# A two-layer attention trunk on one core: a shorter weight scale, a joint maximum over three window groups, and group 2 in pairs of tiles z and z+4

## The chip, the cores and the metric

The kernel runs on one core of one Trainium2 chip. The core has five engines, each with its own queue that is worked off in order: TensorE (PE, matrix products into PSUM), VectorE (DVE), ScalarE (ACT), GpSimd (POOL) and SyncE (SP), which issues nearly all DMAs. An instruction waits at the head of its queue until the semaphores it needs are there, and everything behind it waits too. The metric is device time in microseconds (us) of one execution, lower is better.

## What is computed

A trunk of two layers over 1024 positions of width 1024, with 16 heads of 64. Each layer normalises x, projects it to q, k, v and a gate, attends, multiplies by silu(gate), projects back and adds x. Layer 1 is "forgetting attention" (fox); layer 2 attends in dilated windows, three groups with dilations 1, 4 and 16, and weighs the groups by a softmax over their log-sum-exps.

```python
def reference(x, positions, norm_g, ...):
    cos, sin = rotary_tables(positions)
    for i in range(DEPTH):                       # DEPTH = 2
        h = rms_norm(x, norm_g[i])
        if i % 2 == 0: o, gate = fox_mixer(h, ...)
        else:          o, gate = dsw_mixer(h, cos, sin, ...)
        x = x + (o * silu(gate)) @ w_out

def dsw_mixer(...):      # per group g: q, k = rotary(rms_norm(q)), rotary(rms_norm(k))
    o_g, lse_g = dilated_window_attention(q_g, k_g, v_g, window, dilation)
    wts = softmax(stack(lses), axis=0)
    o = einsum('gbsh,gbshd->bshd', wts, stack(outs))
```

Products are made in float16 with a hi and a lo part of each factor: `xh*wh + xh*wl + xl*wh`, three matmuls for each slice of 128 along the contracted width.

## The kernel before

**Blocks and tiles.** The weights of a projection come in blocks of 384 columns (two heads' q, k and v) by 1024 rows. A block meets the eight tiles of 128 rows of x in `project`, 24 matmuls a tile, into one of three PSUM banks named `pj`. Two tiles make a pair. Layer 1 has three gate blocks, eight of q, k, v and three of the output; layer 2 three gate blocks, then 24 of q, k, v (eight of group 0, then for each of eight head pairs one of group 2 and one of group 1) and three of the output.

**Weights.** A block's weights arrive as four float32 tiles `raw` (L270). `bound` (L272 and on) makes a bound on each: the maximum on DVE for even tiles (L281), the sum of squares on ACT for odd ones (L279, into the scrap tile `jk`); ACT brings both to one tile `vm2` (L284, L285). `scale` (L287 to L304) sums the bounds over the partitions by a matmul (L252, L254), clips (L255), takes the root of a power of two by three integer operations (`root_floor`, L241 to L243), then limits the scale from both sides and tracks the smallest one in `low` (L293 to L300). `split` makes the float16 parts: hi on ACT (L310), lo on DVE (L311); the fourth tile is scaled on POOL (L313), cast on ACT (L314) and its lo part made on POOL (L315).

**The chain of a pair.** After `project` fills a bank, DVE copies q and k to `u` (L433), ACT squares them (L438), ACT and DVE take v to hi and lo (L443, L444); L444 is the last reader and sets the bank free. Then, for the pair: DVE sums the squares (L451) and adds the epsilon (L453, `rs_v`); ACT takes logarithm, exponential and square (L471 to L473), DVE refines the root (L474, L475) and multiplies `u*y` (L477); POOL turns the rotary part (L465 to L468). ACT casts the hi part of the float16 tile `hl` (L479), POOL makes the lo part (L480), DVE copies (L481), and SP sends the whole through a transposing DMA into `qk_t` (L485). There is one `hl`, so the cast also waits for the transposing DMA of the pair before. PE makes the scores of the pair from `qk_t` (L505) 16 slots (two pairs of tiles) after its projection, and its values another 16 slots later (fewer at the end).

**Scores to output in layer 2.** `dsw_pair` masks a score and takes its row maximum in one DVE pass (L970), ACT takes the exponential with that maximum (L971) and casts it (L975), POOL makes the lo part (L976), SP transposes it (L977, `ptt`). Groups 0 and 2 write their unnormalised outputs with the maxima to DRAM (`og_d`, L1083). Group 1 loads them back (`load_cmb`, L1037, L1041), weighs them by their maxima (`weigh`: `mm` on DVE L998, then L1000 to L1004 on POOL and ACT) and combines (`combine`, L1011 to L1019).

**What sets the order.** PE's order is written out by hand: `Flow` holds a queue of slots (four a tile) at which scores, values, loads, bounds, scales and splits come due. The other engines' orders are laid out by the framework's scheduler, which places each instruction where it expects it to be ready; a pair's chain has a raised priority. So a change to what is ready when can change the order of other instructions on the same engine.

## Time and profile before

| | us |
|---|---|
| median of 3 runs (1823.03 to 1827.61) | 1825.76 |
| the profiled execution | 1813.33 |
| its span | 1811.5 |
| PE busy | 1659.2 (92%) |
| DVE busy | 1259.9 (70%) |
| ACT busy | 1068.3 (59%) |
| POOL busy | 872.5 (48%) |

The span runs from the first to the last instruction that the profile holds. The stages of the span are: start and fox gates to 200 us, fox blocks to 570, output of layer 1 and gates of layer 2 to 830, group 0 to 1130, groups 2 and 1 to 1720, output to the end. In the last but one stage a group 2 and a group 1 block together take about 76.6 us. Times of single instructions below are counted from the start of the span. A row of a timeline gives start, length, engine, source line, operation, tiles and shape, and in brackets how long the engine idled before it and what ended that.

### The profile page before, as it was taken

The numbers are of one execution on the slowest core, as the hardware profiler recorded it, in microseconds if no ns is written. First come the engines' busy times: TensorE is split into PE (matmuls) and PEld (weight loads), VectorE is DVE, ScalarE is ACT, GpSimd is POOL, SyncE is SP. The second block draws the span as 40 slices with busy tenths as digits, with TensorE's granted clock in tenths as the row PEclk, the third lists the DMA queues.
The fourth block names the chain that finished last, engine by engine and source line by source line (L and its number), as shares of the span: only waits on it lengthen the run. The fifth ranks groups of instructions, "written<-read, shape, count | busy, mean of one in ns | idle before, by whom it ended". The sixth has DMA issues, their size and how long they took to land.

```text
span 1811.5 us, 38107 instructions
## 1 busy us (share of the span) xinstructions
PE 1659.2 (92%) x13342; PEld 1060.2 (59%) x13342; DVE 1259.9 (70%) x3906; ACT 1068.3 (59%) x2790; POOL 872.5 (48%) x1019
## 2 busy tenths in 40 slices
PE   5899898898888997999999989999899998999999
PEld 3566566566665433756666656656556565565654
DVE  8866677766776557766677786677776777767752
ACT  6555666666666546555666666556555565655630
POOL 4203555555554323125565545556475665646520
PEclk8999999999999998999999999999999999999999
DMA  7334998988889777336777787678676777767742
GB/s 260 122 138 103 191 192 174 168 171 195 191 174 209 205 218 225 109 108 139 141 151 168 149 185 152 138 150 164 153 154 141 157 154 158 161 140 153 190 125 91
DMA packets 658769, 292.88 MB, mean 162 GB/s; under 512 B 510208, under 2 KB 622848, under 8 KB 658576
## 3 DMA queue, kind: packets, MB, share of 16 engines
q1 hardware_dynamic: 658576, 290.44, 69.8%
q8 instruction: 104, 1.70, 0.4%
q14 instruction: 89, 0.73, 0.1%
HBM read 124.35 MB, written 41.22 MB: 91 GB/s over the span
## 4 chain that ended last, share of the span: by engine, by line
PE 36%; DVE 12%; DMA 11%; POOL 5%; issue 5%; ACT 3%; SPq 0%; DVEq 0%; POOLq 0%; ACTq 0%
PE pj L345 24%; PE pj L369 8%; DMA qk_t<-hl 6%; PE s L505 2%; DMA raw<-in_w_dsw 2%; DVE p L970 2%; DVE w L311 2%; DVE hl L481 1%; POOL hl L480 1%; POOL ph L976 1%; DVE pj L451 1%; POOL cmb L1003 1%; DMA ptt<-ph 1%; DVE vm L281 1%; POOL raw L313 1%
## 5 line engine op out<-in xcount | busy, mean ns | idle before, releaser
L345 PE MATMUL pj<-w,xh 128*128 128x384 f16 (+2 forms) x4864 | 1191.2, 329 | 32.7 <-DVE vt L444 18.3
L345 PE MATMUL pj<-w,xl 128*128 128x384 f16 (+2 forms) x2432 | 799.1, 329 | 4.8 <-DVE xl L898 2.6
L345 PEld LDWEIGHTS <-xh 128*128 128x128 f16 x4864 | 473.8, 99 | 322.5 <-issue 48.1
L345 PEld LDWEIGHTS <-xl 128*128 128x128 f16 x2432 | 241.4, 99 | 166.7 <-issue 10.6
L552 POOL TENSOR_TENSOR ph<-p,ph 128x512 f16<-128x512 f32 (+3 forms) x176 | 179.1, 1036 | 190.8 <-ACT ph L549 181.3
L480 POOL TENSOR_TENSOR hl<-u,hl 128x512 f16<-128x512 f32 x128 | 153.9, 1203 | 131.5 <-ACT hl L479 131.3
L976 POOL TENSOR_TENSOR ph<-p,ph 128x768 f16<-128x768 f32 (+2 forms) x96 | 154.0, 1604 | 119.4 <-ACT ph L975 116.1
L505 PE MATMUL s<-qk_t 128*128 128x128 f16 (+1 forms) x1504 | 162.9, 249 | 51.2 <-DMA qk_t<-hl 40.1
L311 DVE SCALAR_TENSOR_TENSOR w<-raw,ws_f,w 128x768 f16<-128x768 f32 (+2 forms) x133 | 181.5, 1379 | 9.6 <-ACT w L310 9.5
L369 PE MATMUL pj<-xh,w 128*128 128x512 f16 x512 | 162.0, 386 | 0.0
L505 PEld LDWEIGHTS <-qk_t 128*128 128x128 f16 x1504 | 113.6, 99 | 70.8 <-DMA qk_t<-hl 44.4
L479 ACT CAST hl<-u 128x512 f16<-128x512 f32 x128 | 78.8, 616 | 120.0 <-DMA qk_t<-hl 90.0
L444 DVE SCALAR_TENSOR_TENSOR vt<-pj,vt 128x128 f16<-128x128 f32 x256 | 73.3, 289 | 109.1 <-ACT vt L443 107.1
L438 ACT ACTIVATE sq<-pj 128x256 f32<-128x256 f32 x256 | 96.2, 376 | 76.7 <-DVE u L433 68.0
L546 ACT ACTIVATE p<-p,acc 128x512 f32<-128x512 f32 (+2 forms) x192 | 108.1, 608 | 36.0 <-DVE acc L745 33.2
L560 PEld LDWEIGHTS <-ptt 128*128 128x128 f16 x1136 | 106.9, 99 | 38.1 <-DMA ptt<-ph 26.0
L369 PEld LDWEIGHTS <-w 128*128 128x128 f16 x768 | 75.2, 100 | 86.2 <-issue 7.0
L549 ACT CAST ph<-p 128x512 f16<-128x512 f32 (+3 forms) x176 | 87.7, 537 | 64.2 <-DMA ptt<-ph 63.8
L310 ACT ACTIVATE w<-raw,ws_f 128x768 f16<-128x768 f32 (+2 forms) x133 | 116.9, 911 | 13.7 <-DVE ws_f L293 13.7
L279 ACT ACTIVATE jk<-raw 128x768 f16<-128x768 f32 (+2 forms) x88 | 72.3, 821 | 85.5 <-DMA raw<-in_w_dsw 43.6
L465 POOL TENSOR_TENSOR ra<-u,cs 128x128 f32<-128x128 f32 x96 | 50.3, 524 | 148.7 <-DVE u L433 69.8
L433 DVE TENSOR_TENSOR u<-pj,gr 128x256 f32<-128x256 f32 x256 | 106.2, 415 | 17.2 <-PE pj L345 16.9
(212 smaller groups left out, 2916.5 us busy)
## 6 DMA issues: line engine op xcount, KB each, us to landing
raw<-in_w_dsw SPq DMA_DIRECT2D x96, 384.0 KB, 3.9
raw<-in_w_fox SPq DMA_DIRECT2D x32, 384.0 KB, 4.2
og_d<-og SPq DMA_DIRECT2D x64, 132.0 KB, 2.8
cmb<-og_d SPq DMA_DIRECT2D x64, 132.0 KB, 2.8
bc<-c_d SPq DMA_DIRECT2D x32, 256.0 KB, 4.6
gs_d<-ge SPq DMA_DIRECT2D x32, 192.0 KB, 2.1
xt<-in_xt SPq DMA_DIRECT2D x16, 256.0 KB, 3.8
gsf<-gs_d SPq DMA_DIRECT2D x64, 64.0 KB, 2.5
```

Of the source, the lines that this page charges most:

```text
L310: nc.scalar.activation(w[:, 0, :, :n], raw, AF.Copy, scale=self.sw)
L311: nc.vector.scalar_tensor_tensor(w[:, 1, :, :n], raw, self.sw, w[:, 0, :, :n], ALU.mult, ALU.subtract)
L345: nc.tensor.matmul(ps[:, :n], a[:, k, cols], w.slab(k, j), start=(k == 0 and i == 0), stop=(k == KT - 1 and i == 2))
L369: nc.tensor.matmul(ps[m], w.slab(k, j)[:, m * P : (m + 1) * P], a[:, k, 512 * b : 512 * (b + 1)], start=(k == 0 and x == 0), stop=(k == KT ...
L433: nc.vector.tensor_mul(u[:, t % 2].rearrange("p (a b) d -> p a b d", a=2), ps[:, : 4 * HD].rearrange("p (a b d) -> p a b d", a=2, b=2), gr ...
L438: nc.scalar.activation(sq[:, t % 2], ps[:, : 4 * HD], AF.Square)
L480: nc.gpsimd.tensor_sub(hl[:, :, :4, 1], u, hl[:, :, :4, 0])
L505: nc.tensor.matmul(s[:, c0 : c0 + cnt * P].rearrange("p (c s) -> p c s", c=cnt), qk[:, i, blk], kk[:, j : j + cnt, e], start=(h == 0), sto ...
L546: nc.scalar.activation(p, p, AF.Exp, bias=acc, scale=-1.0)
L552: (nc.gpsimd if pool_l else nc.vector).tensor_sub(ph[:, e, 1, cols], p, ph[:, e, 0, cols])
L560: nc.tensor.matmul(o[:, e, :], hi, vt[:, j, e, HD:], start=(b == 0), stop=False, skip_group_check=True)
L976: nc.gpsimd.tensor_sub(ph[:, 1], st["p"], ph[:, 0])
```

## The change

- **Scale.** Five small DVE operations a block in place of eight or nine: sum, three integer operations, and one that limits the scale between two numbers that are made once a layer (`lim`). The smallest scale is now taken at the end over all of them (`sws`) and not as a running minimum. ACT writes its bounds straight to `vm2`, and the cast L285 goes.
- **Root.** ACT's logarithm reads the sums of squares in PSUM with scale and bias, not DVE's `rs_v` (which is still made).
- **Gates.** One DVE operation makes the gate's product and its maximum; before there were two.
- **Layer 2.** Group 1's exponentials take the joint maximum of the three groups (`joint_most`), so group 1's output needs no weight of its own and `wt` has two groups. In `combine` the gate is multiplied by the reciprocal of the denominator on POOL (on DVE for the last pair of heads), and two DVE products go. The loads of the other groups' outputs stand nine slots earlier, from two slots after the scores to seven before; `cmb` has four buffers and `gsd` four of its own.
- **Group 2's tiles** are worked in the order 0, 4, 1, 5, 2, 6, 3, 7, so that a write to `og_d` has 256 rows of 132 numbers in place of 128 of 264.

```diff
+def nth_tile(g, t):
+    return t // 2 + 4 * (t % 2) if g == 2 else t
...
-    def root_floor(q):
+    def root_scale(dst, q, k):
         e = q.bitcast(I32)
         nc.vector.tensor_scalar(e, e, 1, 0x7FC00000, ALU.logical_shift_right, ALU.bitwise_and)
-        nc.vector.tensor_scalar(e, e, float(127 << 22), None, ALU.add)
-        nc.vector.tensor_single_scalar(e, e, 0x7F800000, ALU.bitwise_and)
-        return e
+        nc.vector.tensor_scalar(e, e, -1.0, float((k << 23) - (127 << 22)), ALU.mult, ALU.add)
+        nc.vector.tensor_single_scalar(dst.bitcast(I32), e, 0x7F800000, ALU.bitwise_and)
...
-            e = root_floor(spread_sums(self.vm2, KT // 2, 2.0 ** -40, 2.0 ** 60))
...
+            root_scale(f[:, 0:1], spread_sums(self.vm2, KT // 2), 268)
             if self.kind == "qkv":
-                nc.vector.tensor_scalar(t2, self.sw, by[:, ly], 2.0, ALU.mult, ALU.max)
-                nc.vector.tensor_scalar(self.sw, t2, 2.0 ** 30, isx[:, ly], ALU.min, ALU.mult)
-                nc.vector.tensor_scalar(t2, t2, 2.0 ** 30, None, ALU.min)
...
-                nc.vector.tensor_tensor(low[:, ly], low[:, ly], self.sw, ALU.min)
...
+                nc.vector.tensor_scalar(self.sw, f[:, 0:1], m[:, 0:1], m[:, 1:2], ALU.max, ALU.min)
+                nc.scalar.activation(self.eps, self.sw, AF.Square, scale=m[:, 2:3])
...
-        nc.scalar.activation(r, v, AF.Ln)
+        nc.scalar.activation(r, w["ss"], AF.Ln, scale=1.0 / HD, bias=w["eps"])
...
-                nc.vector.scalar_tensor_tensor(e, e, w.inv, ps, ALU.mult, ALU.mult)
-                nc.vector.tensor_reduce(peak[:, layer, h * NT + t : h * NT + t + 1], e, AX.X, ALU.max, apply_absolute_value=True)
+                nc.vector.tensor_tensor_reduce(e, e, ps, w.inv, 0.5, ALU.mult, ALU.max, peak[:, layer, h * NT + t : h * NT + t + 1])
...
-                    nc.scalar.activation(p[:, e], p[:, e], AF.Exp, bias=acc[:, e : e + 1], scale=-1.0)
+                    if joint is None:
+                        nc.scalar.activation(p[:, e], p[:, e], AF.Exp, bias=acc[:, e : e + 1], scale=-1.0)
+            if joint is not None:
+                mm = joint().rearrange("p (i e) -> p i e", e=2)
+                for i in range(2):
+                    p = st["p"][:, at[i] : at[i + 1]].rearrange("p (e k) -> p e k", e=2)
+                    for e in range(2):
+                        nc.scalar.activation(p[:, e], p[:, e], AF.Exp, bias=mm[:, i, e : e + 1], scale=-1.0)
...
+    def joint_most(cmb):
+        nm = cmb[0].rearrange("p g t e d -> p g (t e) d")[:, :, :, 65]
+        mm = cmb[3] = sm.tile([P, N2], F32, name="mm", tag="mm")
+        nc.vector.tensor_reduce(mm, nm.rearrange("p g n -> p n g"), AX.X, ALU.min)
+        return mm
...
-        nc.vector.tensor_mul(o, o, cmb[2][:, 0].unsqueeze(2).broadcast_to([P, N2, HD + 1]))
         nc.vector.tensor_add(o, o, cmb[0][:, 1, :, :, : HD + 1].rearrange("p t e d -> p (t e) d"))
         den = sm.tile([P, N2], F32, name="den", tag="den")
         nc.vector.reciprocal(den, o[:, :, HD])
-        y = o[:, :, :HD]
-        nc.vector.tensor_mul(y, y, den.unsqueeze(2).broadcast_to([P, N2, HD]))
+        (nc.vector if hp == NHP - 1 else nc.gpsimd).tensor_mul(gv, gv, den.unsqueeze(2).broadcast_to([P, N2, HD]))
...
-        nc.vector.tensor_mul(y2, y, gv)
+        nc.vector.tensor_mul(y2, o[:, :, :HD], gv)
...
-                dsw_pair(g, t0, qks, vt, done, get, LSD, LPD)
-                flow.at(flow.now + LSD + 2, lambda hp=hp, t0=t0, cmb=cmb: load_cmb(hp, t0, cmb))
+                flow.at(flow.now + LSD - cfg["lcm"], lambda hp=hp, t0=t0, cmb=cmb: load_cmb(hp, t0, cmb))
+                dsw_pair(g, t0, qks, vt, done, get, LSD, LPD, lambda cmb=cmb: joint_most(cmb))
```

The new code also shifts instructions in the queues. First ACT in a group 1 block of layer 2. The block after it has its weights split here: `w<-raw` are the hi parts, `vt<-ws_f` (after: `vt<-sws`) writes a constant column once a block, `hl<-u` is the cast of a pair's q and k. Before:

```order
L443 ACTIVATE vt<-pj 128x2x64
L310 ACTIVATE w<-raw,ws_f 128x768
L299 ACTIVATE ws_f<-ws_f 128x1
L517 ACTIVATE vt<-ws_f 128x16
L479 CAST hl<-u 128x2x4x64
L314 CAST w<-raw 128x768
L310 ACTIVATE w<-raw,ws_f 128x768 x2
```

After, from the last two hi parts to the cast of the same pair (`rs_y<-rs_y` and `pj<-rs_y` are its exponential and square, `jk` the square passes over the weights loaded next, `p<-p,mm` the next pair's exponentials):

```order
L311 ACTIVATE w<-raw,sws 128x768 x2
L480 ACTIVATE rs_y<-rs_y 128x8
L481 ACTIVATE pj<-rs_y 128x8
L445 ACTIVATE sq<-pj 128x256
L283 ACTIVATE jk,vm_18692<-raw 128x768 x2
L288 ACTIVATE vm_18692<-vm 128x2
L985 ACTIVATE p<-p,mm 128x128 x2
L985 ACTIVATE p<-p,mm 128x256 x2
L450 ACTIVATE vt<-pj 128x2x64
L1019 ACTIVATE wt<-wt 128x8
L487 CAST hl<-u 128x2x4x64
```

The cast moved from right behind the first hi part to behind all hi parts, both square passes and the next pair's exponentials.

DVE at the same place. Before, from the running minimum of the scale (`low`) through the pair's `u*y` (L477) to the first two lo parts of the weights (L311):

```order
L300 TENSOR_TENSOR low<-low,ws_f 128x1
L475 SCALAR_TENSOR_TENSOR pj<-pj,rs_y 128x8
L477 TENSOR_TENSOR u<-u,pj 128x512
L444 SCALAR_TENSOR_TENSOR vt<-pj,vt 128x2x64
L311 SCALAR_TENSOR_TENSOR w<-raw,ws_f,w 128x768
L433 TENSOR_TENSOR u<-pj,gr 128x256
L1011 TENSOR_TENSOR ob<-ob,wt 128x260
L311 SCALAR_TENSOR_TENSOR w<-raw,ws_f,w 128x768
```

After, the rows that end with the same pair's `u*y` (L485); its three lo parts of the weights (L312) and the first two score passes stand ahead of them:

```order
L977 ISA p,cmb<-s_17794,band 128x256
L977 ISA cmb 128x1
L977 ISA p,cmb<-s_17794,band 128x256
L977 ISA cmb 128x1
L1031 RECIPROCAL den<-ob 128x4
L458 TENSOR_REDUCE pj<-sq 128x8
L483 SCALAR_TENSOR_TENSOR pj<-pj,rs_y 128x8
L285 TENSOR_REDUCE vm<-raw 128x1
L1011 TENSOR_REDUCE mm<-cmb 128x4
L461 TENSOR_SCALAR rs_v<-pj,ws_f 128x8
L1035 TENSOR_TENSOR y_17858<-ob,gsd 128x256
L485 TENSOR_TENSOR u<-u,pj 128x512
```

`u*y` moved from ahead of the first lo part to behind the third, behind the next pair's score passes (L977) and its sum (L458), and behind a pass over newly loaded weights (L285).

ACT in a group 0 block. Before, from the first hi part to the pair's cast:

```order
L310 ACTIVATE w<-raw,ws_f 128x768
L299 ACTIVATE ws_f<-ws_f 128x1
L517 ACTIVATE vt<-ws_f 128x16
L473 ACTIVATE pj<-rs_y 128x8
L438 ACTIVATE sq<-pj 128x256
L443 ACTIVATE vt<-pj 128x2x64
L314 CAST w<-raw 128x768
L310 ACTIVATE w<-raw,ws_f 128x768 x2
L479 CAST hl<-u 128x2x4x64
```

After, from the last two hi parts to the cast of the same pair:

```order
L311 ACTIVATE w<-raw,sws 128x768 x2
L445 ACTIVATE sq<-pj 128x256
L450 ACTIVATE vt<-pj 128x2x64
L479 ACTIVATE rs_y<-pj,ws_f 128x8
L480 ACTIVATE rs_y<-rs_y 128x8
L481 ACTIVATE pj<-rs_y 128x8
L1098 COPY og<-ob 128x4x65
L445 ACTIVATE sq<-pj 128x256
L979 ACTIVATE p<-p,og 128x256 x3
L283 ACTIVATE jk,vm_14050<-raw 128x768
L979 ACTIVATE p<-p,og 128x256
L487 CAST hl<-u 128x2x4x64
```

The pair's root (L479 to L481) now follows the hi parts, and the cast follows the next pair's four exponentials and one square pass over the weights.

More of the change, by code (lines that the diff above doesn't have):

```diff
@@ L276, in bound @@
             raw = self.raw[i][:, :, : self.n]
-            if i % 2:
+            if i not in cfg["most"]:
                 jk = sb.tile([P, 2, self.n], F16, name="jk", tag="jk", bufs=1)
-                nc.scalar.activation(jk, raw, AF.Square, accum_out=self.vm[:, i : i + 1])
+                with nc.allow_low_precision(reason="a bound within a factor of two is enough"):
+                    nc.scalar.activation(jk, raw, AF.Square, accum_out=self.vm2[:, i : i + 1])
             else:
                 nc.vector.tensor_reduce(self.vm[:, i : i + 1], raw, AX.XY, ALU.max, apply_absolute_value=True)
-            if i == KT // 2 - 1:
-                v = [a.rearrange("p (a b) -> p a b", b=2) for a in (self.vm, self.vm2)]
-                nc.scalar.activation(v[1][:, :, 0], v[0][:, :, 0], AF.Square)
-                nc.scalar.copy(v[1][:, :, 1], v[0][:, :, 1])
+            if i == max(cfg["most"]):
+                c = slice(0, i + 1, 2)
+                nc.scalar.activation(self.vm2[:, c], self.vm[:, c], AF.Square)
@@ L422, in y_scale_end @@
         c = sy[:, layer : layer + 1]
-        nc.vector.tensor_mul(c, c, low[:, layer : layer + 1])
+        lw = sm.tile([P, 1], F32, name="lw", tag="yg")
+        nc.vector.tensor_reduce(lw, sws[:, layer, : rank[layer]], AX.X, ALU.min)
+        nc.vector.tensor_mul(c, c, lw)
     def heads_begin():
@@ L940, in trunk, with dsw_pair @@
     written = set()
[L942 removed]
+    def dsw_pair(g, t0, qks, vt, done, get, LSD, LPD, joint=None):
         mask = masks.get(g)
```

72 lines of the change are left out of this document (37 added, 35 removed).

## The prediction

> **What bounds the kernel now.** I read the busy time by stage first, then TensorE's waits, then one period of layer 2 instruction by instruction.
>
> ```profile
> 200.00:570.00 370.00, 326.26 (x3326) 0.96 0.87 183
> 830.00:1130.00 300.00, 288.59 (x2483) 0.99 0.76 157
> 1130.00:1720.00 590.00, 555.27 (x4375) 0.98 0.72 155
> ...
> sum 1811.50, PE 1659.23 PEld 1060.24 DVE 1259.93 ACT 1068.25 POOL 872.49; mean PE 276.54 PEld 176.71 DVE 209.99 ACT 178.04 POOL 145.42
> ```
>
> The rows are stretches of the span: bounds, length, PE busy, granted clock. The first is the eight fox blocks, the second layer 2's eight group 0 blocks, the third the alternating group 2 and group 1 blocks. PE is busy for 1659 of 1811.5 us and its order is fixed, so the end moves only by PE's waits and its clock. It idles 43.7 us in the fox blocks, 11.4 in group 0, 34.7 in groups 2 and 1. DVE, at 1260 us, has slack on average; taking work from it gains only where PE waits for it.
>
> ```profile
> PE s L505 <- DMA qk_t<-hl: 40.1, 31, 4.7
> ...
> PE pj L345 <- DVE vt L444: 18.3, 10, 2.9
> PE nb L595 <- DVE dg L590: 9.5, 1, 9.5
> ...
> PE pj L345 <- DVE ge L536: 7.8, 5, 4.5
> ```
>
> Columns: total wait, times, longest. The first row is scores that wait for the transposed q and k. That transpose stands at the end of a chain over four engines: root and `u*y` on DVE, hi cast on ACT, lo part on POOL, copy on DVE, then SP's DMA. **The order in which this chain stands in the engines' queues matters more than DVE's total.**
>
> ```profile
> 1193.84 0.62 PE L505 MATMUL s<-qk_t 128*128 128x128 f16 x8
> 1196.98 0.48 PE L345 MATMUL pj<-w,xh 128*128 128x384 f16 x2 [2.51 <-DVE vt L444]
> ...
> 1208.67 0.62 PE L505 MATMUL s<-qk_t 128*128 128x128 f16 x8 [1.50 <-DMA qk_t<-hl]
> ```
>
> This is one group 1 block: start, length, instruction, wait before it. Call the pair scored at 1193.84 pair A, the one at 1208.67 pair B. A's score came with no wait; then a bank (2.51) and B (1.50) were waited for, 4.0 us in all.
>
> **What the change removes.**
>
> ```profile
> L537 DVE TENSOR_REDUCE peak<-ge 128x1 f32<-128x384 f32 (+1 forms) x48 | 24.0, 501 | 0.8
> L300 DVE TENSOR_TENSOR low<-low,ws_f 128x1 f32<-128x1 f32 x32 | 24.1, 754 | 0.0
> L1011 DVE TENSOR_TENSOR ob<-ob,wt 128x260 f32<-128x260 f32 x32 | 13.7, 428 | 4.9 <-PE ob L562 4.5
> ```
>
> These three groups alone are 61.8 us of DVE time that disappears: the gates' second pass, the running minimum of the scale, one product of the combine. At the gates PE waits for DVE's pass (7.8 us) and at the start for `dg`; shorter queues there should return some 6 us. Bounds: nothing, if the same chain through ACT's four passes stays last, and 13 us, if the gates' waits and half of the `dg` wait go.
>
> **What it moves: pair A's chain.** The new orders show that the scale, now five DVE operations, is ready earlier than before, and that the weight splits took the places of A's chain. In a group 1 block A's cast (L487) now stands behind three splits, two square passes over newly loaded weights and the next pair's four exponentials; A's `u*y` (L485) stands behind the splits, four score passes, the next pair's sum and two bound passes. I walk the new order with the durations of before.
>
> ```profile
> 1179.20 0.16 DVE L254 TENSOR_REDUCE v<-pj 128x1 f32<-128x4 f32 x1
> ...
> 1182.40 0.20 DVE L296 TENSOR_SCALAR ws_f<-ws_f,isx 128x1 f32<-128x1 f32 x1
> ...
> 1183.18 0.69 DVE L477 TENSOR_TENSOR u<-u,pj 128x512 f32<-128x512 f32 x1
> ...
> 1188.34 1.52 DVE L481 COPY hl<-hl 128x512 f16<-128x512 f16 x1
> ...
> 1191.01 0.94 DVE L281 TENSOR_REDUCE vm<-raw 128x1 f32<-128x768 f32 x1
> ...
> 1192.80 0.68 DVE L451 TENSOR_REDUCE pj<-sq 128x8 f32<-128x512 f32 x1
> ```
>
> ```profile
> L311 DVE SCALAR_TENSOR_TENSOR w<-raw,ws_f,w 128x768 f16<-128x768 f32 (+2 forms) x133 | 181.5, 1379 | 9.6 <-ACT w L310 9.5
> ...
> L970 DVE CUSTOM_DVE_ANT_0 p<-s,band 128x256 f32<-128x256 f32 (+1 forms) x256 | 85.1, 374 | 5.8 <-PE s L505 5.6
> ```
>
> Before: the bound's sum at 1179.20, the multiplier at 1182.60, A's `u*y` done at 1183.87, its copy held in the queue until 1189.86, the score at 1193.84. After, the sum stands in the same place (behind four score passes, which wait for PE), and the multiplier comes about 1.2 us sooner. But the second split's hi part still waits for ACT's casts, so the second split ends near 1188.2, where the copy's row begins. From there DVE has one gate product (0.4), a bound pass (0.94), one addition (0.4), the third split (1.38): 1191.3. Then four score passes with readouts (4 x 0.45 = 1.8), the next sum (0.68), a second bound pass (0.94) and small ones (0.8): 1195.5; A's `u*y` ends near 1196.2.
>
> ```profile
> 1183.98 0.61 ACT L479 CAST hl<-u 128x512 f16<-128x512 f32 x1
> ...
> 1190.78 0.91 ACT L971 ACTIVATE p<-p,cmb 128x256 f32<-128x256 f32 x2 [0.28 <-DVE cmb L970]
> 1191.59 0.83 ACT L279 ACTIVATE jk<-raw 128x768 f16<-128x768 f32 x1
> ```
>
> ```profile
> 1181.33 1.65 POOL L976 TENSOR_TENSOR ph<-p,ph 128x768 f16<-128x768 f32 x1
> 1182.93 1.06 POOL L1003 TENSOR_TENSOR cmb<-cmb,wt 128x520 f32<-128x520 f32 x1
> ...
> 1186.23 1.16 POOL L480 TENSOR_TENSOR hl<-u,hl 128x512 f16<-128x512 f32 x1
> 1187.35 2.36 POOL L315 TENSOR_TENSOR w<-raw,w 128x768 f16<-128x768 f32 x1
> ```
>
> ```profile
> 1189.92 1.28 SPq L485 DMA_TRANSPOSE qk_t<-hl  x1
> ```
>
> ```profile
> raw<-in_w_dsw SPq DMA_DIRECT2D x96, 384.0 KB, 3.9
> ```
>
> ACT's second square pass needs a load that goes out only after the third split: 1191.3 + 3.9 = 1195.2, and 0.83 for the pass: 1196.0. Four exponentials take some 1.6 (0.91 for the two wide ones, less for the narrow), a `vt` and a `wt` 0.5: 1198.1. Then A's cast, 0.61: 1198.7. POOL has a weighting (1.06) ahead of A's lo part (1.16), and it waits for that `wt`: 1200.4. The copy takes 0.3 without a neighbour on POOL: 1200.7. From the issue at 1189.92 to the score at 1193.84 lie 3.9 us: **A's score could start near 1204.6, where PE wants it at 1193.84: a wait of 10.8 us.** The lower bound takes the loads as always there and DVE 2.5 us ahead: `u*y` at 1193.7, cast, lo part and copy in sequence to 1195.8, score at 1199.7, a wait of 5.9. I take 9, nearer to the end that the walk gives. While PE waits 9 us, the other engines catch up, so I strike the 4.0 us that PE waits now. Net +5 a block (bounds +1.9 and +6.8), in the seven of these blocks that load a further block: +35 (13 to 48).
>
> **The clock after the wait.**
>
> ```profile
> 1197.00:1206.60 9.60, 9.60 (x53) 0.82 0.46 106
> 1209.20:1217.10 7.90, 7.90 (x56) 1.00 0.59 124
> 1081.10:1090.90 9.80, 9.80 (x50) 0.78 1.03 175
> ```
>
> Each stretch is the two tiles after a wait: of 2.51 us, of 1.50, and of 4.7 (the longest in the row of waits). The first and last run 1.7 to 1.9 us longer at a granted clock of 0.82 and 0.78. A wait of 9 us is not in this trace; since 4.7 costs hardly more than 2.5, I count 1.9 as before, and nothing net. [...]
>
> **Groups 0 and 2.**
>
> ```profile
> 956.98 0.28 DVE L481 COPY hl<-hl 128x512 f16<-128x512 f16 x1
> ...
> 1230.00 0.28 DVE L481 COPY hl<-hl 128x512 f16<-128x512 f16 x1
> ```
>
> ```profile
> 960.99 0.40 PE L505 MATMUL s<-qk_t 128*128 128x128 f16 x4 [0.19 <-DMA qk_t<-hl]
> ...
> 1234.96 0.34 PE L505 MATMUL s<-qk_t 128*128 128x128 f16 x3 [0.18 <-DMA qk_t<-hl]
> ```
>
> Here `u*y`, cast and lo part ran between the splits, and the copy waited in DVE's queue behind the score passes. After, `u*y` comes behind the passes: `u*y` 0.69, cast 0.61 and lo part 1.16 follow instead of lying beside them, 2.5 us more, less the 0.75 of L300 that DVE saves: +1.7. In group 0 the copy's end at 957.26 plus 3.9 is later than PE wants it, so all of it shows: 8 x 1.7 = +14 (0 if DVE's lead eats it, 31 if a square pass's load adds 2 us). In group 2, 1230.28 + 3.9 leaves 0.8 us: 8 x 0.9 = +7 (0 to 18).
>
> **At nothing.** The fox blocks, 43.7 us of waits now: there too the splits pass A's chain, which costs, and the logarithm no longer waits for DVE, which gains; I see no sign and bound it by -12 and +12. The product of gates and denominators on POOL, 28 of some 0.9 us (L315's 2.36 and L481's 1.52 above, which overlap in time, show that neighbours on DVE and POOL can lengthen each other), lies off A's chain unless POOL is late. The Trainium skill (SBUF — State Buffer, "The single rule") has VectorE and GpSimd exclude each other at one shared pair of ports, the later one blocked for the whole instruction: by that each such product could hold up a DVE product with two SBUF inputs, at most an estimated 28 x 0.9 = 25 us of DVE time, off PE's path by the same sum. Four combine loads a period instead of two now stand on SP directly behind the write they read, but 14 slots ahead of their use; nothing.
>
> **Sum.** +35 + 14 + 7 + 0 - 6 = +50. The profiled execution took 1813.3 us, 12.4 under the median of the runs shown; 1813.3 + 50 = 1863 on its footing, 1825.8 + 50 = **1876 us** on the median's, which I forecast.
>
> **The rivals.** *Relief* (ends faster): DVE's smaller load is what PE lacked, and real queues run ahead of my walk, so that A's copy still ends by 1190. Then the bank waits (18.3), the gates' (7.8) and the slow stretches behind seven bank waits (7 x 1.7 = 12) go: -38, or 1788; with half of it 1807. For it: nearly every bank wait in layer 2 is for DVE. Against it: A's `u*y` stands in DVE's queue behind a pass over scores that PE makes at a fixed point. It decides at a copy by 1190.0; mine ends at 1200.7. *Exchange* (no change): the lower bound in group 1, 7 x 1.9 = +13, nothing in groups 0 and 2, and -6 at the gates and -7 in fox: 1826. *Cold clock* (slower still): the loss grows with the wait, 1.7 for 2.51, so 6.1 for 9 us, 4.4 more: +31, 1907. The 0.78 after 4.7 us speaks against it. That the operations are not gone is no rival: the orders show them gone.
>
> **How the numbers follow.** Forecast 0.53, relief 0.24, exchange 0.13, cold clock 0.10. The measurement of this kernel tells about 0.3%, 5.5 us. Faster: relief and a little of exchange, 0.25; same: the rest of exchange, 0.12; slower 0.63. The forecast's own range is 1840 to 1905 (the bounds of single terms will not all fall together). Low end 1805, which leaves out half of relief; high end 1905, which leaves out half of cold clock.
>
> **What would show it.** PE's waits for `qk_t` rising from 40 to some 110 us, in the stretch of groups 2 and 1 above all; a wait of 6 to 11 us before one score of each group 1 block, its releaser the transpose; the waits for `vt` L444's successor nearly gone; A's cast on ACT directly behind four exponentials and a square pass that waited for a load. If instead these scores come without a wait, the walk is wrong and relief holds; if the wait is there but nearer to 6, the load was in time. If group 0's idle time stays near 11 us, that term is wrong.

## The result, and the profile after

| | before | after |
|---|---|---|
| median of 4 runs (lowest to highest), us | 1826.23 (1823.03 to 1827.61) | 1931.94 (1928.02 to 1935.92) |
| ratio, 95% interval | | 1.058 (1.0555 to 1.0608) |
| the profiled execution, us | 1813.33 | 1933.24 |

The change makes the kernel **slower by 105.7 us**. The forecast was slower, at 1876; the time is above its range of 1840 to 1905. The two traces differ by more than the medians, by 119.9 us, since before's profiled execution lies 12.9 under its median and after's 1.3 over.

The page of after, busy time by engine:

```profile
span 1931.4 us, 37869 instructions
PE 1686.9 (87%) x13342; PEld 1067.8 (55%) x13342; DVE 1200.7 (62%) x3667; ACT 1078.4 (56%) x2746; POOL 882.2 (46%) x1047
```

DVE did get its load off: 1201 us where it had 1260. PE, which has the same matmuls, is busy 28 us longer (a lower clock), and idles 244.5 us instead of 152.3. PE's waits in after, total, times, longest:

```profile
PE s L513 <- DMA qk_t<-hl: 86.7, 33, 5.3
PE pj L346 <- DVE u L485: 35.2, 10, 5.6
...
PE pj L346 <- DVE vt L451: 16.6, 17, 3.8
PE nb L602 <- DVE dg L597: 12.8, 1, 12.8
...
PE pj L346 <- DVE peak L544: 9.3, 7, 2.6
```

Scores wait twice as long for the transposed q and k (86.7 against 40.1), and a row that stood at 0.9 us before is now the second: a projection that waits for a PSUM bank until `u*y` (L485) has been made.

To see where, both spans are cut at the same events, the first score of the first fox block, of layer 1's last, of group 0 and of groups 2 and 1. The rows are the stretch, its length, then each engine's busy time, PE's granted clock, DMA. Before, group 0 and then groups 2 and 1:

```profile
809.30:1122.90 313.60, 302.19 (x2594) 198.62 (x2595) 228.57 (x709) 206.60 (x558) 176.98 (x208) 0.99 0.74 154
1122.90:1701.60 578.70, 545.15 (x4285) 348.39 (x4286) 422.20 (x1479) 340.10 (x1024) 343.09 (x474) 0.98 0.71 153
```

After, the fox blocks, then the same two:

```profile
154.50:537.30 382.80, 329.64 (x3284) 227.15 (x3281) 248.97 (x823) 249.02 (x604) 190.82 (x188) 0.96 0.85 172
...
826.10:1192.60 366.50, 316.56 (x2593) 202.49 (x2593) 240.00 (x672) 211.95 (x550) 175.75 (x209) 0.95 0.64 133
1192.60:1821.40 628.80, 557.40 (x4285) 351.52 (x4285) 385.49 (x1348) 337.98 (x1010) 367.12 (x501) 0.95 0.66 141
```

**Group 0 costs 52.9 us more, groups 2 and 1 cost 50.1 more.** In each a part is idle time (49.9 against 11.4 in group 0, 71.4 against 33.6 in groups 2 and 1) and the rest is clock (PE busy 14.4 and 12.3 longer for the same matmuls). The fox blocks take 16 us longer than in before's trace (366.4 there), but that stretch was short in that one execution: e7 and e9 below, which leave the fox blocks as they were, took 377 and 374 there. That leaves 6 to 9 us in fox, whose cause is open. The stages not shown differ by at most 4.4 us.

### A group 2 block of after

A name has to be set right first. Before, the prediction's pair A is scored at 1193.84, and this is DVE's first pass over that score:

```profile
1199.44 0.28 DVE L970 CUSTOM_DVE_ANT_0 p<-s,par 128x128 f32<-128x128 f32 x1
1199.65 0.08 DVE L970 DVE_READ_ACCUMULATOR2_ANT og<- 128x1 f32 x1
```

The mask `par` belongs to group 2 alone (L937), and the row maximum goes to `og`, a tile that group 1 doesn't have. So the block that the prediction walks as one of group 1, and whose queues are shown ahead of it, is one of group 2, and the blocks that it prices as group 2 are group 1's. The exponentials with `mm` ahead of the cast are those of the group 1 block before. The walk stands, since its rows are those of the block that it walks. From here on the names are the right ones.

The three engines of the pair's chain between two waits of PE. DVE:

```profile
1267.99 0.95 DVE L285 TENSOR_REDUCE vm<-raw 128x1 f32<-128x768 f32 x1 [0.87 <-DMA raw<-in_w_dsw]
...
1269.41 0.68 DVE L485 TENSOR_TENSOR u<-u,pj 128x512 f32<-128x512 f32 x1
...
1274.37 0.81 DVE L489 COPY hl<-hl 128x512 f16<-128x512 f16 x1
```

ACT:

```profile
1269.41 0.84 ACT L283 ACTIVATE jk<-raw 128x768 f16<-128x768 f32 x1 [2.79 <-DMA raw<-in_w_dsw]
...
1270.35 1.48 ACT L985 ACTIVATE p<-p,mm 128x128 f32<-128x128 f32 x4
...
1271.98 0.61 ACT L487 CAST hl<-u 128x512 f16<-128x512 f32 x1
```

POOL, and PE's two waits of this block:

```profile
1272.16 1.05 POOL L1021 TENSOR_TENSOR cmb<-cmb,wt 128x520 f32<-128x520 f32 x1 [2.85 <-ACT wt L1019]
1273.17 1.16 POOL L488 TENSOR_TENSOR hl<-u,hl 128x512 f16<-128x512 f32 x1
```

```profile
1270.14 0.80 PE L346 MATMUL pj<-w,xh 128*128 128x384 f16 x2 [4.76 <-DVE u L485]
1280.16 1.03 PE L513 MATMUL s<-qk_t 128*128 128x128 f16 x8 [3.93 <-DMA qk_t<-hl]
```

This is the chain that the forecast walked: `u*y` behind a bound pass that waits for a load, the cast behind a square pass that waits for a load and four exponentials, the lo part behind a weighting. PE waits 8.7 us in the block where 9 were forecast, but in two places, and this is the longest of the seven such blocks: PE idles 6.9 us in them on average, before 4.4. The root's small operands lie in spare columns of the pair's second PSUM bank (`pj` in L483 and L485), so a late `u*y` also holds a bank back from the next projection. The forecast saw only the score's wait.

### A group 0 block of after

DVE, ACT and POOL around the first pair of a block, and PE's score of it:

```profile
986.98 2.45 DVE L312 SCALAR_TENSOR_TENSOR w<-raw,sws,w 128x768 f16<-128x768 f32 x1
...
996.11 0.67 DVE L485 TENSOR_TENSOR u<-u,pj 128x512 f32<-128x512 f32 x1
...
999.80 2.20 DVE L489 COPY hl<-hl 128x512 f16<-128x512 f16 x1 [0.77 <-POOL hl L488]
```

```profile
996.69 0.84 ACT L283 ACTIVATE jk<-raw 128x768 f16<-128x768 f32 x1 [0.87 <-DMA raw<-in_w_dsw]
...
997.93 0.60 ACT L487 CAST hl<-u 128x512 f16<-128x512 f32 x1
```

```profile
986.49 2.13 POOL L990 TENSOR_TENSOR ph<-p,ph 128x1024 f16<-128x1024 f32 x1
...
998.61 1.16 POOL L488 TENSOR_TENSOR hl<-u,hl 128x512 f16<-128x512 f32 x1 [2.92 <-DMA raw<-in_w_dsw]
999.73 2.13 POOL L990 TENSOR_TENSOR ph<-p,ph 128x1024 f16<-128x1024 f32 x1
```

```profile
1005.98 0.83 PE L513 MATMUL s<-qk_t 128*128 128x128 f16 x8 [4.33 <-DMA qk_t<-hl]
```

The chain is in sequence, as forecast, but it holds three things that the forecast's +1.7 us did not count. A split took 2.45 us beside a POOL pass (the stage's 24 splits take 43.7 us in all, before 34.5). ACT waited for a load. And the copy, 0.28 us before, took **2.20** (1.84 to 2.21 in seven of the eight blocks): it is ready 0.07 us after POOL has begun its 2.13 us pass and ends 0.14 after that pass.

### The profile page after: what moved, and what is told of

Read it like the earlier page. It is cut to its first block, busy times and chain, and to the rows that moved or that the text cites. A ratio compares the mean times of both kernels' runs of the same rounds, so it can differ in the third digit from the quotient of the medians.

```text
span 1931.4 us, 37869 instructions
## 1 busy us (share of the span) xinstructions
PE 1686.9 (87%) x13342; PEld 1067.8 (55%) x13342; DVE 1200.7 (62%) x3667; ACT 1078.4 (56%) x2746; POOL 882.2 (46%) x1047
## 4 chain that ended last, share of the span: by engine, by line
PE 37%; DMA 17%; DVE 9%; ACT 7%; issue 6%; POOL 5%; SPq 1%; DVEq 0%; POOLq 0%; ACTq 0%
PE pj L346 26%; PE pj L370 7%; DMA qk_t<-hl 6%; DMA ptt<-ph 5%; DMA raw<-in_w_dsw 4%; PE s L513 3%; DVE w L312 2%; POOL hl L488 2%; ACT w L311 1%; DVE hl L489 1%; POOL w L316 1%; POOL ph L559 1%; ACT ph L556 1%; DVE p L977 1%; ACT p L553 1%
## 5 line engine op out<-in xcount | busy, mean ns | idle before, releaser
L346 PE MATMUL pj<-w,xh 128*128 128x384 f16 (+2 forms) x4864 | 1204.9, 332 | 67.4 <-DVE u L485 35.2
L559 POOL TENSOR_TENSOR ph<-p,ph 128x512 f16<-128x512 f32 (+3 forms) x176 | 172.2, 997 | 205.5 <-ACT ph L556 201.7
L513 PE MATMUL s<-qk_t 128*128 128x128 f16 (+1 forms) x1504 | 168.9, 255 | 103.8 <-DMA qk_t<-hl 86.7
L488 POOL TENSOR_TENSOR hl<-u,hl 128x512 f16<-128x512 f32 x128 | 148.4, 1159 | 214.6 <-ACT hl L487 193.9
L990 POOL TENSOR_TENSOR ph<-p,ph 128x768 f16<-128x768 f32 (+2 forms) x96 | 160.4, 1671 | 59.2 <-ACT ph L989 56.4
L312 DVE SCALAR_TENSOR_TENSOR w<-raw,sws,w 128x768 f16<-128x768 f32 x96 | 137.6, 1448 | 27.6 <-ACT w L311 27.3
L473 POOL TENSOR_TENSOR ra<-u,cs 128x128 f32<-128x128 f32 x96 | 48.9, 510 | 192.6 <-DVE u L440 71.4
L489 DVE COPY hl<-hl 128x512 f16<-128x512 f16 x128 | 66.3, 518 | 100.2 <-POOL hl L488 98.7
L451 DVE SCALAR_TENSOR_TENSOR vt<-pj,vt 128x128 f16<-128x128 f32 x256 | 74.1, 289 | 84.9 <-ACT vt L450 84.0
```

What stands on the lines that cost most here:

```text
L312: nc.vector.scalar_tensor_tensor(w[:, 1, :, :n], raw, self.sw, w[:, 0, :, :n], ALU.mult, ALU.subtract)
L346: nc.tensor.matmul(ps[:, :n], a[:, k, cols], w.slab(k, j), start=(k == 0 and i == 0), stop=(k == KT - 1 and i == 2))
L488: nc.gpsimd.tensor_sub(hl[:, :, :4, 1], u, hl[:, :, :4, 0])
L513: nc.tensor.matmul(s[:, c0 : c0 + cnt * P].rearrange("p (c s) -> p c s", c=cnt), qk[:, i, blk], kk[:, j : j + cnt, e], start=(h == 0), sto ...
L559: (nc.gpsimd if pool_l else nc.vector).tensor_sub(ph[:, e, 1, cols], p, ph[:, e, 0, cols])
L990: nc.gpsimd.tensor_sub(ph[:, 1], st["p"], ph[:, 0])
```

## The experiments

The scheduler's order can be summed up in one number a stage: behind how many of a block's three lo splits the first pair's `u*y` stands in DVE's program order (in all but a layer's first block; the first group 2 block has the number of group 0). e6 and e8 have the order of after. From the orders and the traces (the first score of a stage to that of the next):

| kernel | behind, fox / group 0 / 1 / 2 | fox, us | group 0, us | groups 2 and 1, us | median, us (runs) |
|---|---|---|---|---|---|
| before | 1 / 1 / 1 / 0 | 366 | 314 | 579 | 1826.2 (4) |
| after | 3 / 3 / 3 / 3 | 383 | 366 | 629 | 1931.9 (4) |
| e2, scale alone | 3 / 3 / 3 / 1 | 377 | 370 | 586 | 1893.4 (1) |
| e3, root alone | 3 / 1 / 1 / 1 | 375 | 316 | 573 | 1821.8 (1) |
| e4, all but scale | 3 / 1 / 1 / 3 | 377 | 317 | 618 | 1867.6 (1) |
| e7, joint and pairs | 1 / 1 / 1 / 1 | 377 | 314 | 586 | 1837.4 (4) |
| e1, scale due later | 0 / 0 / 0 / 0 | 401 | 335 | 589 | 1884.2 (4) |
| e5, scale held by data | 0 / 0 / 0 / 0 | 387 | 322 | 607 | 1874.7 (4) |
| e12, held and later | 3 / 0 / 0 / 0 | 383 | 322 | 591 | 1851.5 (4) |

Groups 2 and 1 alternate, so their stage has to be cut by block, here from a block's first projection matmul to that of the next. A group 1 block and the group 2 block behind it, first before, then after, then e2:

```profile
1132.30:1167.40 35.10, 35.10 (x277) 22.49 (x275) 24.77 (x87) 21.62 (x68) 18.00 (x28) 1.00 0.66 144
1167.40:1209.10 41.70, 37.69 (x299) 23.87 (x297) 31.27 (x108) 23.51 (x71) 28.78 (x40) 0.96 0.77 153
...
1204.70:1243.20 38.50, 35.28 (x277) 22.50 (x274) 23.57 (x82) 22.29 (x69) 20.48 (x28) 1.00 0.58 126
1243.20:1291.00 47.80, 39.10 (x300) 24.47 (x299) 27.18 (x96) 22.48 (x67) 28.45 (x40) 0.93 0.64 133
...
1207.10:1244.90 37.80, 35.25 (x276) 22.51 (x274) 23.66 (x82) 21.96 (x69) 19.69 (x27) 1.00 0.62 137
1244.90:1284.70 39.80, 37.58 (x300) 23.82 (x299) 29.24 (x102) 23.19 (x68) 26.39 (x37) 0.96 0.71 153
```

| mean length of seven blocks, us | before | after | e2 | e4 | e7 |
|---|---|---|---|---|---|
| group 1, all but the last | 35.5 | 38.7 | 38.4 | 35.6 | 36.1 |
| group 2, all but the first | 41.6 | 45.2 | 39.7 | 46.4 | 42.1 |

In layer 2 a number of 3 costs: 57 us in group 0 (e2), some 3 us a block in group 1 (e2 against before) and some 4 in group 2 (e4 against e7, which has the same joint maximum and pairs). That groups 2 and 1 lose only 7 us in e2 is a net: its group 2 blocks, at 1, are 2 us shorter than before's, at 0. Of the 39 that they lose in e4, 7 come without the 3 (e7). In fox the 3 costs nothing that shows (e3: 375, where e7 and e9 with a 1 have 377 and 374). A low number is not free either: e1 and e5, which bring it to 0 by other means, pay elsewhere.

### e2, e3, e4: which part moves the order

e2 has the scale's operations alone on the kernel before, e3 the logarithm that reads PSUM alone, e4 all of the change but the scale. The edits, in short:

```diff
 e2 (on before)
-                nc.vector.tensor_scalar(t2, self.sw, by[:, ly], 2.0, ALU.mult, ALU.max)
...
+                nc.vector.tensor_scalar(self.sw, f[:, 0:1], m[:, 0:1], m[:, 1:2], ALU.max, ALU.min)
 e3 (on before)
-        nc.scalar.activation(r, v, AF.Ln)
+        nc.scalar.activation(r, w["ss"], AF.Ln, scale=1.0 / HD, bias=w["eps"])
 e4 (on after)
-            root_scale(f[:, 0:1], spread_sums(self.vm2, KT // 2), 268)
+            e = root_floor(spread_sums(self.vm2, KT // 2, 2.0 ** -40, 2.0 ** 60))
```

> Of the change only the five-operation scale, on the kernel before (the bounds, logarithm, gates and layer 2 as before). The order has pair A's u*y behind all three lo parts in the fox and group 0 blocks and in every second block of groups 2 and 1. Queue order: group 0 about 45 us a block as in the changed kernel (+56), fox about +10, groups 2 and 1 about half of their +48: 1890 to 1925 us. The new operations: the scale alone has fewer operations than before, so 1826 or less.

> Of the change only the logarithm that reads the sums in PSUM, on the kernel before. The order moves u*y behind the splits in the fox blocks alone. Queue order: loss in the fox blocks (up to the changed kernel's +13), nothing in groups 0, 2 and 1: 1825 to 1842 us. New operations (a read of PSUM by the logarithm is what costs): layer 2's blocks slow too, by several us each: over 1860.

> The change without the new scale (bound, logarithm, gates, joint maximum and group 2's pairs stay). The order moves u*y behind the splits in the fox blocks and in every second block of groups 2 and 1; not in group 0. Queue order: group 0 stays at 37.7 us a block, fox about +10, groups 2 and 1 about half of +48: 1840 to 1865. New operations: all of the joint maximum's and the logarithm's loss is there, so about 1870 to 1930.

Group 0, then groups 2 and 1, of e2; then the same of e4:

```profile
825.70:1196.00 370.30, 317.59 (x2593) 204.40 (x2593) 237.62 (x673) 206.36 (x558) 175.86 (x211) 0.94 0.61 131
1196.00:1782.00 586.00, 545.56 (x4284) 348.75 (x4284) 407.94 (x1403) 340.21 (x1025) 350.05 (x471) 0.98 0.69 150
```

```profile
820.40:1137.50 317.10, 302.56 (x2592) 198.99 (x2592) 230.54 (x708) 211.47 (x549) 176.41 (x208) 0.99 0.73 153
1137.50:1755.40 617.90, 553.62 (x4285) 350.29 (x4285) 409.33 (x1425) 336.63 (x1012) 364.36 (x503) 0.96 0.67 145
```

The two halves of the loss come apart. Five scale operations in place of eight or nine, by themselves, cost group 0 all of it (+57) and groups 2 and 1 only 7. The rest of the change costs group 0 nothing that shows (+3.5) and groups 2 and 1 39, with the 3 in the group 2 blocks, where e2 has 1. That e2 has less work on DVE and is 67 us slower rules out DVE's load as the cause. The logarithm costs nothing: 1821.8, with fox at 3. In total e2 is where queue order expected it; e4 came 2.6 us above its range, and the loss in fox that e3 was to show did not come.

### e1: the scale due four slots later

```diff
-wscale=8, wsplit=(10, 16, 22, 12))
+wscale=12, wsplit=(13, 18, 22, 14))
```

> The whole change, with every operation of it, but the scale of the next block's weights comes due at slot 12 of a block and not 8, its first two splits at 13 and 14 and not 10 and 12. In the new order each block has pair A's u*y on VectorE ahead of all three lo parts again. Theory 'queue order': the 106 us come from pair A's chain standing behind the splits, so group 0 goes back from 45.9 to about 37.7 us a block, the periods of groups 2 and 1 from 83 to 75 or 76, PE's waits for the bank that u*y releases (35.2 us) go: 1800 to 1830 us in all. Rival 'the new operations' (the logarithm reading PSUM, the gate product on GpSimd, exponentials that wait for the joint maximum): the cost stays whatever the order, over 1890 us.

1884.22, ratio 1.032 (1.0302 to 1.0337): not quite half of the loss is back, which is neither of the two expected ranges. Groups 2 and 1 return 40 us and run at clock 0.99:

```profile
153.80:554.40 400.60, 332.70 (x3284) 229.49 (x3281) 250.25 (x822) 248.46 (x600) 195.65 (x188) 0.93 0.80 165
...
1180.30:1769.50 589.20, 543.03 (x4289) 347.43 (x4286) 386.99 (x1349) 345.47 (x1007) 373.61 (x502) 0.99 0.71 151
```

The fox blocks lose 18 instead, and group 0 returns only 31 of 53. With the splits due later the bank waits for `vt` (L451) rise from 16.6 to 46.9 us in all. One slot for all stages is the wrong tool.

### e5: the order held by data

The limits of the scale are read through the first pair's refined root, times zero, so the splits can't be placed ahead of it. One small DVE operation a block is added; the rest is as in after.

```diff
-                nc.vector.tensor_scalar(self.sw, f[:, 0:1], m[:, 0:1], m[:, 1:2], ALU.max, ALU.min)
...
+                m = sm.tile([P, 2], F32, name="lim2", tag="lim2")
+                nc.vector.scalar_tensor_tensor(m, y[:, 0, 0:2], 0.0, self.m[:, 0:2], ALU.mult, ALU.add)
+                self.limit(m)
```

> The whole change; added is one small operation a block on VectorE: the limits of the next block's scale are read through pair A's refined root (y times 0 plus the limits), so no split can start before A's root is done. Everything stays due where the change has it. The order has A's u*y ahead of all three lo parts in every block that is followed by a block of q, k and v. Queue order: group 0 at 37.5 to 39 us a block, the periods of groups 2 and 1 at 71 to 76 us (one of the two blocks ran at 34.75 without a wait where only the other was turned), no wait of PE for u*y of some 5 us: 1795 to 1830 us. Against it, lateness of the loads: the splits come about 1 us later than before and the bound and the next splits with them, so a wait for vt or for the weights takes the place: 1850 to 1890, as with the scale at slot 12. The new operations: over 1890.

1874.66, ratio 1.029 (1.0262 to 1.0324). Group 0 took 322.5, with 18.0 us idle: 44 of its 53 us are back, with every removed operation still removed. With the order the collisions go too: the copy takes 0.54 there and the 24 splits 34.4 in all. Groups 2 and 1 went from 629 to 607 only, at the same order 0 as e1's 589. So there order is not all, and the total lies where late splits and loads were expected to hold it (1850 to 1890). That the hold itself delays the splits, which e1 with its later slots does not pay, is a reading of the two, not a separate test.

### e6: the root's operands out of PSUM

Is the wait for the bank a cost of its own? Here the two small operands lie in SBUF, so `u*y` holds no bank.

```diff
+        w["a"], w["y"] = (sm.tile([P, 2, 4], F32, name=k, tag=k) for k in ("rs_a", "rs_z"))
```

> The changed kernel, but the two scratch arrays of the root (a and y, 128 x 8 each) lie in SBUF and not in the spare columns of the projection's bank; u*y then no longer keeps a bank. Bank theory (part of the 106 us is PE waiting for a bank that only u*y releases): PE's waits with u*y as releaser (35.2 us) go to nothing, the waits for qk_t rise by less, 1900 to 1925 us. Rival (the transposed q and k set the time alone, and the bank's wait only comes first): the waits for qk_t take over all of it, 1928 to 1936.

1967.32, slower than after, which neither theory expected. PE's longest waits, and the small operations, mean ns of one behind the total:

```profile
PE s L514 <- DMA qk_t<-hl: 170.9, 32, 12.5
```

```profile
L486 DVE TENSOR_TENSOR u<-u,rs_z 128x512 f32<-128x512 f32 x128 | 94.8, 740 | 4.3
...
L483 DVE SCALAR_TENSOR_TENSOR rs_a<-rs_a,rs_v 128x8 f32<-128x8 f32 x128 | 52.5, 410 | 37.6 <-ACT rs_a L482 36.9
```

The bank waits are gone, and the score waits rose by more (84 us against 35), to 9.5 to 12.5 in group 2: the forecast's walk gave 10.8. That fits a wait for the bank that is the same lateness of the chain, met earlier, with a stop of PE there that lets the chain catch up. It does not show it, because the edit also made the chain slower. Of the 128 operations of L483, 71 took 0.16 us, as on PSUM operands (0.17, L482 of after); the other 57 took 0.72 on average, and each of these began while a POOL pass ran. On PSUM operands none took more than 0.18. So the spare PSUM columns were the better place, and how much of the 84 us is the missing stop is open.

### e8: the copy made in a way that POOL doesn't slow

```diff
-        nc.vector.tensor_copy(hl[:, :, 4:], hl[:, :, 2:4, ::-1])
+        for i in range(2):
+            nc.vector.tensor_reduce(hl[:, i, 4:], hl[:, i, 2:4, ::-1].unsqueeze(4), AX.X, ALU.max)
```

> The changed kernel, but the copy at the end of a pair's chain (2.20 us in each group 0 block of the changed kernel's trace, 0.28 before, started 0.07 us after a 2.13 us pass of GpSimd) is written as two maximum reductions over one element each, which move the same numbers. Port theory (the copy waits for GpSimd to finish, because the two engines exclude each other; the Trainium skill, SBUF — State Buffer, 'The single rule', says that a reduction on this chip never does): the two take 0.6 to 0.9 us in group 0 beside the same pass, pair A's score comes 1.3 to 1.6 us earlier there, a block takes 43.5 to 44.3 us and not 45.6, 1912 to 1924 us in all. Rival (the copy is long for its own data or its access, or PE waits for something else at the same time): no shorter, 1928 to 1936.

```profile
L490 DVE TENSOR_REDUCE hl<-hl 128x256 f16<-128x256 f16 x256 | 95.1, 413 | 96.5 <-POOL hl L488 95.0 <-DMA og_d<-og 1.3
```

Two reductions of 0.41 each in place of one copy, and none of the 256 is slowed (0.40 to 0.42). Group 0 took 351.5 where after took 366.5, so the copy's collision is worth about 15 of the 53 us. Group 0 did as port theory expected, the total did not (1933.15, ratio to before 1.062 (1.0564 to 1.0665)): groups 2 and 1, whose copies were mostly short, took 5 us more, and fox 5. The Trainium skill (SBUF — State Buffer, "The single rule") says that a copy may take the port pair that VectorE shares with GpSimd and is then shut out until GpSimd's instruction ends, and that a reduction never contends on this chip. The 2.20 us copy and the steady 0.41 agree with both.

### e7, e9: the joint maximum and group 2's pairs

e7 has these alone on the kernel before; e9 is e7 with the product of gate and 1/denominator on DVE for all heads.

```diff
-        (nc.vector if hp == NHP - 1 else nc.gpsimd).tensor_mul(gv, gv, den.unsqueeze(2).broadcast_to([P, N2, HD]))
+        nc.vector.tensor_mul(gv, gv, den.unsqueeze(2).broadcast_to([P, N2, HD]))
```

> Of the change the joint maximum, the combine, the earlier loads and group 2's pairs, on the kernel before (its scale, bounds, logarithm and gates). The order has A's u*y behind the first lo part in every block of layer 2. Queue order: these parts alone cost nothing and relieve VectorE, periods of groups 2 and 1 between 70 and 76.6 us: 1780 to 1826. New operations (product on GpSimd, wait for the joint maximum, four loads a period behind their writes): periods over 78, so over 1838.

> As the run with the joint maximum and group 2's pairs alone (1837.4), but the product of gate and denominator's reciprocal is on VectorE for all heads and not on GpSimd. GpSimd theory (that product delays the lo parts behind it, or VectorE's passes beside it): 1822 to 1830, periods of groups 2 and 1 down from 79 to 77 us. Rival (the rest of the joint maximum costs, the wait of the exponentials above all): 1835 to 1845.

e7: 1837.38, ratio 1.007 (1.0048 to 1.0100). e9: 1835.30 over 10 runs, ratio 1.007 (1.0044 to 1.0092). This part alone costs 12 to 13 us; e7 lies between its two expected ranges, e9 in that of the rival. Groups 2 and 1 take 586 and 585, where before, e3 and e10, which lack this part, took 573 to 583. e9 has the product on DVE, and its order puts `u*y` back to 0 in group 2 as before. The cost stays, so neither the product on POOL nor the place of `u*y` explains it by itself. What it is was not found.

### e10, e11: is there a gain in the small parts?

e10 has root, gate product and bound alone on the kernel before; e11 adds e8's reductions.

```diff
-                nc.vector.scalar_tensor_tensor(e, e, w.inv, ps, ALU.mult, ALU.mult)
-                nc.vector.tensor_reduce(peak[:, layer, h * NT + t : h * NT + t + 1], e, AX.X, ALU.max, apply_absolute_value=True)
+                nc.vector.tensor_tensor_reduce(e, e, ps, w.inv, 0.5, ALU.mult, ALU.max, peak[:, layer, h * NT + t : h * NT + t + 1])
```

> Of the change the logarithm, the gates and the bounds' direct write, on the kernel before; scale, joint maximum and group 2's pairs as before. The order has u*y behind the splits in the fox blocks only. My term for the gates (6 us), if right, and the 4 us that the logarithm alone seemed to gain: 1812 to 1819. If the logarithm's gain was scatter and the gates' waits are set by ACT: 1822 to 1828.

> As the run with logarithm, gates and bounds, with the pair's copy as two reductions. In the kernel before, that copy took 1.13 or 1.52 us in two of eight pairs of groups 2 and 1, 0.28 elsewhere. Port theory: 0.5 to 1 us a block where it was long, and a slow clock stretch saved here and there: 5 to 15 us below the run without it. Rival: the reductions are longer than a free copy (0.6 against 0.28), and where no pass of GpSimd runs beside, that is lost: 0 to 8 us above it.

e10: 1822.62 over 10 runs, ratio 1.000 (0.9974 to 1.0029), where the forecast's term for the gates was -6. Its row `peak` in PE's waits is 5.4 us, where before had 7.8 for its first pass (`ge`): 2.4 us, lost in the scatter, since after itself has 9.3 there. That is the second of the two expected ranges. e11: 1862.65, ratio 1.022 (1.0171 to 1.0270), 40 us slower than e10 from two reductions of 0.41 in place of a copy that is mostly 0.28; groups 2 and 1 took 600 instead of 583. Neither expectation allowed for that. The edit is all that differs, so it costs the 40; by which path was not followed up.

### e12: each stage with the remedy that helped it

Held by data in group 0, due later in groups 2 and 1 (e1's slots, but the second split at 16 and not 18).

```diff
-            flow.at(s0 + cfg["wscale"], blocks[i + 1].scale)
+            blocks[i + 1].held = 17 <= i < 25
+            flow.at(s0 + (12 if i >= 25 else cfg["wscale"]), blocks[i + 1].scale)
```

> The whole change, with the order put back by the means that worked in each stage alone: in the group 0 blocks the next scale's limits wait for pair A's root (blocks of 38.5 us in that run), in the blocks of groups 2 and 1 the next scale comes due at slot 12 and its first splits at 13 and 14 (589 us from the first group 2 score to the last block, against 629 in the changed kernel and 579 in the trace before); fox and gate blocks as changed. Queue order: both gains add up, 57 + 40 = 97 us less at most; group 0 at 38 to 39 us a block, groups 2 and 1 at 585 to 595: 1838 to 1855. Rival (each gain only moved the wait into the next stage, or part of the loss lies in the other stages): over 1870.

1851.54, ratio 1.014 (1.0107 to 1.0174): **80 of the 106 us are back**, with all arithmetic of the change in place, and within the range expected of queue order. Fox, group 0, groups 2 and 1:

```profile
155.50:538.50 383.00, 325.08 (x3283) 225.26 (x3281) 248.12 (x823) 249.10 (x604) 190.88 (x188) 0.97 0.86 172
826.00:1147.60 321.60, 304.39 (x2593) 198.98 (x2592) 218.53 (x677) 211.92 (x548) 179.84 (x208) 0.98 0.72 152
1147.60:1738.30 590.70, 546.51 (x4291) 348.69 (x4288) 387.47 (x1349) 345.01 (x1007) 374.04 (x502) 0.98 0.70 150
```

Group 0 keeps 8 us and groups 2 and 1 keep 12, against before's trace; e7 by itself cost 7 in groups 2 and 1. The remainder, in fox, at the end and in the scatter between executions, stays open. No version run here is faster than before by more than the scatter: e10 is level, and e3's 1821.8 is a single run.

## Why the prediction was right in sign and short in size

| step of the prediction | forecast, us | measured, us |
|---|---|---|
| the prediction's group 1 (in truth 2), the first pair's chain behind the splits | +35 | +25 (seven blocks of 45.2, before 41.6) |
| its group 2 (in truth 1), the same | +7 | +22 (seven blocks of 38.7, before 35.5) |
| group 0, the same | +14 (0 to 31) | +53 (after), +57 (e2) |
| the clock after the waits | 0 | +27, contained in the rows above |
| fox | 0 | nothing from the order (e3); 6 to 9 open |
| gates | -6 | 0 (e10) |

- **Right: the mechanism.** The chain of a block's first pair moved behind the splits, and its place, not DVE's load, decides. e2 (less work, slower) and e5 (the work of after and one small operation more in another order, 57 us faster than after) show it from both sides. Relief, the rival that ends faster, would have needed the first pair's copy early; in the group 2 block shown PE wants the score 3.93 us before 1280.16, and the copy would have to end 3.9 us (the forecast's time from issue to score) ahead of that, by 1272.3; it starts at 1274.37.
- **Right in sum, partly by luck: groups 2 and 1.** The sum was +42, and after has +50, made up otherwise. The walked block was to wait 9 us for one score, less the 4.0 of before. Blocks of its kind wait 6.9 less 4.4, first 3.6 to 5.6 for the bank and then 1.5 to 3.9 for the score, and 1.0 of their 3.6 us more is clock. The other kind was to lose 0.9 a block, because "1230.28 + 3.9 leaves 0.8 us". But the row at 1234.96 that the prediction shows waits 0.18 us for `qk_t`, so nothing was left there, and it lost 3.2. Of the marks that were given, the waits for `qk_t` came to 86.7 and not 110, and they rose most in group 0 (from 10.6 to 38.5), not in groups 2 and 1 (from 13.9 to some 31). That the waits for `vt` would nearly go was wrong (16.6 against 18.3).
- **Wrong: the group 0 term,** "`u*y` 0.69, cast 0.61 and lo part 1.16 follow instead of lying beside them, 2.5 us more, less the 0.75 of L300: +1.7". It is +6.6 a block (52.9 / 8), and that is where the forecast is short: 39 us. Of the 6.6, 4.8 is idle time and 1.8 clock (14.4 / 8). The working took the durations of the old neighbourhood. In the new one the copy meets a POOL pass (1.9 more; e8: 15 us of the stage), splits meet POOL passes (9 us over the stage: 43.7 for the 24 of them, before 34.5) and ACT waits for a load; the last two were not tested apart. The forecast had named the neighbours on DVE and POOL, but only for the new product, not for the copy that moved.
- **Wrong: no net clock.** The price of a wait was about right: group 0 has eight more waits of 3.8 to 5.3 us than before, and PE's busy time there is 14.4 us longer, 1.8 for each. The count was wrong, since "as before, and nothing net" leaves these waits out. Nor does each wait of 2 or 3 us cost this, as the relief rival took it: before, only four of the seven bank waits in groups 2 and 1 were followed by a slow stretch. After the 3.37 us wait that ends at 1285.29 before there was none, and after the one of 4.33 that ends at 1005.98 in after there was (the last but two numbers are the granted clock):

```profile
1285.30:1294.90 9.60, 9.60 (x80) 6.35 (x81) 5.75 (x27) 5.03 (x16) 3.88 (x4) 1.00 0.51 109
...
1006.00:1015.60 9.60, 9.60 (x53) 5.60 (x54) 4.65 (x18) 5.33 (x15) 4.96 (x6) 0.82 0.69 134
```

- **Wrong: -6 at the gates.** The stated lower bound, nothing, holds.
- The cold clock rival (1907) did not come as priced: its loss was to grow with the wait, and in e6, whose score waits in group 2 are 9.5 to 12.5 us, PE is busy for 556.8 us in groups 2 and 1, in after for 557.4.

## What to carry to other kernels

When a scheduler lays out the queues by readiness, a shorter chain for unhurried work (here weight scales) can overtake a critical one: look at where the critical chain stands in the new order before counting what was removed. Price a moved instruction with its new neighbours, since a copy that took 0.28 us took 2.20 beside a POOL pass that began 0.07 us earlier. And count the waits, not only their sum: the eight more waits of 3.8 to 5.3 us in group 0 cost 14 us of clock on top.

## What the runs showed of the hardware that was not expected

- A 128x512 float16 copy on DVE: 0.28 to 0.30 us where no POOL pass was running as it began (78 of after's 128), 2.20 when a POOL pass of 2.13 us had begun 0.07 us before. As two reductions it took 0.41 each, whatever POOL did.
- A DVE operation over 128x8 took 0.16 us on SBUF operands (e6, 71 of 128) and 0.17 on PSUM ones (after). On SBUF operands 57 took longer, 0.72 on average, all of them begun while a POOL pass ran; on PSUM operands none did.
- In layer 2's projections of after, each wait of PE of 3.6 us or more was followed by a slow stretch, worth 1.3 to 2.8 us by the granted clock. Waits of 2.3 to 2.7 us were followed by one of 1.7 or by none, and before even one of 3.37 by none.
